# Drains of the matmul banks ahead of weight splits, and the attention bursts of the odd layer three eighths later in their unit

## The chip, the cores and the metric

The kernel runs on one core of one Trainium2 chip. The metric is the time of one execution in microseconds on the device; the kernel before has a median of 748.38 us of three runs (748.29 to 749.49). TensorE is called PE in the rows below, VectorE DVE, ScalarE ACT, GpSimd POOL and SyncE SP.

## The reference

Two layers over 256 tokens of 1024 features, in fp32, each an attention and a squared-ReLU MLP, with RMS norms and residual adds. The even layer joins neighbourhood attention (8 heads) and latent attention (8 heads), the odd layer mixes three dilated windows for 16 heads:

```python
for layer in range(DEPTH):                       # DEPTH = 2
    xn = rms_norm(x, norm_mix[layer])
    if layer % 2 == 0:
        x = x + even_mixer(xn, ev_w_in[e], ev_rpb[e], ev_q_norm[e], ev_w_uq[e],
                           ev_kv_norm[e], ev_w_ukv[e], ev_w_o[e], cos_r, sin_r)
    else:
        x = x + odd_mixer(xn, od_w_in[o], od_w_o[o], cos_f, sin_f)
    x = x + sq_relu_mlp(rms_norm(x, norm_mlp[layer]), mlp_w1[layer], mlp_w2[layer])
return rms_norm(x, norm_final)

def odd_mixer(xn, w_in, w_o, cos_f, sin_f):
    hcat = (xn @ w_in).reshape(b, s, DIL_GROUPS, 3, DIL_HEADS, HEAD_DIM)
    q = apply_rope(hcat[:, :, :, 0], cos_f, sin_f)
    k = apply_rope(hcat[:, :, :, 1], cos_f, sin_f)
    v = hcat[:, :, :, 2]
    return dilated_attention(q, k, v) @ w_o      # masked softmax per window, mixed by denominators
```

## The kernel before

The four stages follow one another: the even attention layer (about 0 to 110 us), its MLP (to 300), the odd attention layer (to 565) and the last MLP.

Each product of two fp32 matrices is done as three or two matmuls of halves: every operand is split into a rounded part and the rest. The weights come from HBM by SyncE's DMAs into four buffers `raw`. A weight is then split in four pieces: ScalarE casts (`whi`, line 176), VectorE subtracts (`wlo`, line 177), into three buffers. `weight()` loads four weights ahead and splits two ahead. The function `split` does the same two steps for activations, and so lines 176 and 177 also stand for the results of attention: `oa` and `ob` are the two halves of what a mix leaves in a bank.

TensorE's results lie in eight PSUM banks, four of tag "acc" and four of tag "w". A matmul into a new bank waits until the last result in that bank has been emptied. What empties banks (the *drains*) runs on ScalarE and VectorE as well, behind and between the weight pieces: `joined` (lines 193 and 194) copies and adds the two halves of a projection, line 932 copies turned probabilities (`pts`), lines 848, 851 and 852 scale the values (`v`), line 666 copies the latent layer's values (`vml`), line 722 or 736 copies turned probabilities of the even layer.

A scheduler puts the instructions of each engine in order. Each has a priority that falls with its place in the code; `tc.high_priority(n)` raises what stands under it by n places. TensorE's order follows the written code for the most part.

The odd layer has eight units. A unit is 12 *half steps* (`qk_steps`: two batches of rows by three blocks f by two halves of the depth, a new weight at half steps 0, 4 and 8) and four *value steps* (two weights). Beside the matmuls of unit u stands one *burst*, that of unit u - 1: `mix` of unit u - 3 (lines 942 and 947), `turn` of unit u - 2's first probabilities (12 transpositions, line 929, into two banks), `scores` of unit u - 1 (lines 201 and 907) and between its two kinds the other `turn`. A burst so opens five "acc" banks one after the other, and the half steps open one each two. The softmax of these scores (lines 913 to 917) follows on VectorE and ScalarE.

Of the kernel before, what the change touches and what calls it, by code (L numbers as in the profile page):

```python
# [38 lines left out]
SPLIT_AHEAD = 2  # L39
WPARTS = 4  # L40
NORM_PRIO = 300


@with_exitstack
def trunk(ctx, tc, a, out):
# [27 lines left out]
    def halves(z):  # L73

        return (z[:, 0, :], z[:, 1, :]) if len(z.shape) == 3 else (z[:, :, 0, :], z[:, :, 1, :])
# [99 lines left out]
    def split(hi, lo, src, eng=None):  # L175
        a = nc.scalar.copy(hi, src).ins  # L176
        return a, (eng or nc.vector).tensor_tensor(lo, src, hi.bitcast(F32), op=ALU.subtract).ins  # L177
# [25 lines left out]
    def weave(main, side, lead=0):  # L203

        done = 0
        for i, step in enumerate(main):
            step()
            while done < len(side) and done * (len(main) - lead) < (i + 1 - lead) * len(side):
                side[done]()
                done += 1  # L210

    def tok(t):
        return slice(t * P, (t + 1) * P)
# [258 lines left out]
    def even(ep):  # L472
# [124 lines left out]
        def qk_steps(c):  # L597
            hold = {}

            def step(f, half):  # L600
                if not hold:
                    hold["w"], hold["p"] = weight(), bank("acc" if c else "w")
                (wh, wl), pq = hold["w"], two(hold["p"])
                for k in range(4 * half, 4 * half + 4):
                    ws = slice(k * 256 + f * P, k * 256 + f * P + P)
                    mm3(pq[:, f], wh[:, ws], wl[:, ws], *halves(xT[:, k]), k == 0, k == KT - 1)
                if f == 1 and half == 1:
                    qk[c] = pair_tile(ep, 2, "qk", 2, "qk")
                    q32 = scratch([2, T], "q32")
                    nc.vector.tensor_tensor(q32, pq, both, op=ALU.mult)  # L610
                    split(*halves(qk[c]), q32)

            return [lambda f=f, h=h: step(f, h) for f in range(2) for h in range(2)]
# [13 lines left out]
        def query_steps():  # L627
            hold = {}

            def step(m):  # L630
                if not hold:
                    hold["w"] = latent_weight("q", "mq")
                wh, wl = hold["w"]
                pq = two(bank("acc"))
                for j in range(2):
                    for k in range(2):
                        c = slice(k * D + (2 * m + j) * P, k * D + (2 * m + j + 1) * P)
                        mm3(pq[:, j], wh[:, c], wl[:, c], cT_h[:, k], cT_l[:, k], k == 0, k == 1)
                q32 = scratch([2, T], "qm")
                nc.vector.tensor_tensor(q32, pq, turns, op=ALU.mult)  # L640
                split(*halves(mT["q"][:, 2 * m:2 * m + 2]), q32)

            return [lambda m=m: step(m) for m in range(4)]

        def key_value_steps():
            hold = {}

            def keys(b):
                if not hold:
                    hold["w"] = latent_weight("k", "mk")  # L650
                    for j, rows in enumerate((slice(64, P), slice(0, 64))):
                        nc.sync.dma_start(by_parity(mT["k"])[rows, j].bitcast(F32), cT[rows, 3].bitcast(F32).unsqueeze(1).broadcast_to([64, 4, 2, T]))
                wh, wl = hold["w"]
                pk = two(bank("acc"))
                for m in range(2):
                    c = slice((2 * b + m) * P, (2 * b + m + 1) * P)
                    mm3(pk[:, m], wh[:, c], wl[:, c], cT_h[:, 2], cT_l[:, 2], True, True)
                for j, rows in enumerate((slice(0, 64), slice(64, P))):
                    o = by_parity(mT["k"])[rows, j, 2 * b:2 * b + 2]
                    split(o[:, :, 0], o[:, :, 1], pk[rows])  # L660

            def values(t):
                wh, wl = hold["w"]
                pv = bank("acc")
                mm3(pv, cT_h[:, 2, tok(t)], cT_l[:, 2, tok(t)], wh[:, 512:D], wl[:, 512:D], True, True)
                nc.any.tensor_copy(out=vml[:, t], in_=pv)

            return [lambda b=b: keys(b) for b in range(2)] + [lambda t=t: values(t) for t in range(NT)]

# [55 lines left out]
        def turn_pair(hp):  # L725

            pt, pts = [bank("w") for _ in range(2)], [scratch([8, 64], "pts") for _ in range(2)]
            for t in range(NT):
                pp = probs.pop(2 * hp + t)
                for b in range(4):  # L730
                    for r in range(2):
                        rows, at = slice(64 * r, 64 * r + 64), slice((4 * t + b) * 64, (4 * t + b) * 64 + 64)
                        nc.tensor.transpose(pt[r][:, at], pp[rows, b // 2, (b % 2) * P:(b % 2 + 1) * P], ident[rows, rows])
                turned[2 * hp + t] = [(slice(64 * r, 64 * r + 64), lambda b, t=t, r=r: pts[r][:, 4 * t + b, :]) for r in range(2)]
            for r in range(2):
                nc.any.tensor_copy(out=pts[r], in_=pt[r].rearrange("p (b n) -> p b n", b=8))

        def mix(*pairs):
            kind, _, hp = items[2 * pairs[0]]
            if mixed[kind] is None:  # L740
                mixed[kind] = quarter_pair("ob")
            v = (vna, vml)[kind]
            pvo = bank("acc" if pairs[0] < 2 else "w")
            for i, m in enumerate(pairs):
                for t in range(NT):
                    pts, o = turned.pop(2 * m + t), i * T + t * P
                    for own, block in pts:
                        for kk in range(NT):
                            for j in range(2):
                                h = 2 * (hp + i) + j  # L750
                                nc.tensor.matmul(pvo[64 * j:64 * j + 64, o + own.start:o + own.stop], v[:, kk, h * 64:(h + 1) * 64],  # L751
                                                 block(2 * j + kk), start=kk == 0, stop=kk == NT - 1)
            n = len(pairs)
            split(*halves(mixed[kind][:, hp:hp + n]), pvo[:, 0:n * T].rearrange("p (i n) -> p i n", i=n))

        def attention():

# [57 lines left out]
    def odd(op, xT, s):  # L815
# [15 lines left out]
        def value_steps(d):  # L831

            wt, acc = [], {}

            def gemm(i, half):
                if len(wt) <= half:
                    wt.append(weight())
                if half == 0:
                    acc[i] = bank("acc")
                pq = acc[i]  # L840
                wh, wl = wt[half]
                for k in range(4):
                    ws = slice(k * 384, k * 384 + 384)
                    kk = 4 * half + k
                    mm3(pq[:, 0:384], xh[:, kk, tok(i)], xl[:, kk, tok(i)], wh[:, ws], wl[:, ws], kk == 0, kk == KT - 1)
            def out(i):
                pq, ri = acc[i], column(r[0], i)
                nc.vector.tensor_scalar(d["v0"][:, i, :], pq[:, 0:P], ri, None, ALU.mult)
                for c in range(2):
                    rows = slice(64 * c, 64 * c + 64)  # L850
                    nc.scalar.activation(d["v12"][0:64, 2 * i + c, :], pq[rows, P:2 * P], AF.Copy, scale=ri[rows])  # L851
                    nc.scalar.activation(d["v12"][64:P, 2 * i + c, :], pq[rows, 2 * P:3 * P], AF.Copy, scale=ri[rows])  # L852

            return [lambda i=i, h=h: gemm(i, h) for i in range(NT) for h in range(2)], [lambda i=i: out(i) for i in range(NT)]

        def qk_steps(d):
# [4 lines left out]
            def gemm(b, f, half):  # L861
# [6 lines left out]
                    ws = slice((f * KT + k) * P, (f * KT + k + 1) * P)  # L868
                    mm2(pq, wh[:, ws], wl[:, ws], xT[:, k], k == 0, k == KT - 1)
                if half == 1:  # L870
                    joined(s[:, f], pq)
                if f == 1 and half == 1:
                    rope(b, s)

# [45 lines left out]
        def turn(u, i, tag):  # L920
# [7 lines left out]
                        rows = slice(64 * r, 64 * r + 64)  # L928
                        nc.tensor.transpose(pt[r][:, at], pp[rows, b * P:(b + 1) * P], ident[rows, rows])
            pts = turned[u, i] = op.tile([P, 6, P], F32, tag="pts", name="pts", bufs=2)  # L930
            for r in range(2):
                nc.any.tensor_copy(out=pts[:, :, 64 * r:64 * r + 64], in_=pt[r][:, 0:384].rearrange("p (b n) -> p b n", b=6))

        def mix(u, d, out_tag):
            pvo = bank(out_tag)
            for i in range(NT):
# [6 lines left out]
                for c in range(2):  # L943
                    qs = slice(64 * c, 64 * c + 64)
                    for j in range(2):
                        cs = slice(64 * j, 64 * j + 64)
                        nc.tensor.matmul(pvo[cs, at + 64 * c:at + 64 * c + 64], d["v12"][:, 2 * i + c, cs], pts[:, 3 * j + 2, qs],
                                         start=False, stop=c == 1)
            split(*halves(mixed[u // 4][:, u % 4]), pvo[:, 0:T])

        units = [unit_tiles(0)]
        d = units[0]
# [27 lines left out]

        for u in range(1, 8):
            units.append(unit_tiles(u))
            placed = {3 if u == 1 else 1: burst(u - 1)}
            if u == 7:
                placed[13] = burst(7)
            beside(qk_steps(units[u]) + all_values(units[u]), placed)
# [119 lines left out]
```

## Time and profile before

| what | value |
|---|---|
| median of three runs | 748.38 us |
| the profiled execution | 749.12 us, its span 747.3 us |
| PE busy | 731.1 us, 98% |
| DVE busy | 537.2 us, 72% |
| ACT busy | 464.2 us, 62% |
| DMA | mean 183 GB/s |

Times in the rows are microseconds from the span's start. A timeline row gives start, duration, engine, source line, operation, what it writes and reads, the count, and in brackets the idle time ahead of it with what ended it. Neighbours of one kind are merged in one row.

### The profile page before, as it was taken

To read this page: it belongs to the slowest core of one execution; us is meant where nothing else is said; L and a number is where in the kernel's file an instruction comes from. 1 tells how busy PE (TensorE), PEld (TensorE's weight loads), DVE (VectorE), ACT (ScalarE), POOL (GpSimd) and SP (SyncE) were. 2 spreads that over 40 slices of the span, in tenths; PEclk is the share of its full clock that TensorE was granted. 3 is DMA by queue.
4 is the path that set the end of the run, shared out by engine and by line. 5 is a ranking of instruction groups with operands and counts; after the bars stand their busy time and mean duration, and the time that the engine had idled before them with its cause. 6 is when DMAs were issued, how large, how long until landed. Compare 5 with 4: busy or idle time off the path is not lost.

```text
span 747.3 us, 12828 instructions
## 1 busy us (share of the span) xinstructions
PE 731.1 (98%) x4932; PEld 641.7 (86%) x4932; DVE 537.2 (72%) x1111; ACT 464.2 (62%) x1043; POOL 6.0 (1%) x16
## 2 busy tenths in 40 slices
PE   8998999999999999999999999999999999999996
PEld 5898998888888888888989889888898888888885
DVE  6698869665665666998777777787669665665664
ACT  7689967544544547766686676866757554554541
POOL 0100000000000000000000000000000000000000
PEclk9999999999999999999999999999999999999998
DMA  8966334555556545675545665456364655455501
GB/s 279 344 209 219 117 123 157 200 195 197 183 184 210 184 142 169 212 247 177 190 167 173 199 210 172 159 189 200 99 242 170 210 184 187 175 202 180 182 33 56
DMA packets 28108, 136.89 MB, mean 183 GB/s; under 512 B 4496, under 2 KB 7056, under 8 KB 14992
## 3 DMA queue, kind: packets, MB, share of 16 engines
q1 hardware_dynamic: 27760, 135.81, 53.5%
q8 instruction: 38, 0.62, 0.3%
q10 hardware_dynamic: 288, 0.28, 0.1%
q14 instruction: 22, 0.18, 0.1%
HBM read 127.68 MB, written 1.05 MB: 172 GB/s over the span
## 4 chain that ended last, share of the span: by engine, by line
PE 85%; ACT 7%; DVE 3%; DMA 2%; issue 1%; SPq 0%; POOLq 0%; POOL 0%; DVEq 0%
PE w L186 16%; PE acc L180 13%; PE acc L181 13%; PE acc L182 13%; PE acc L186 10%; PE w L187 8%; PE acc L187 5%; ACT whi L176 3%; DVE wlo L177 1%; DMA raw<-in_w_v 1%; PE w L751 1%; DMA bias<-in_rpb 1%; ACT v L851 1%; ACT v L852 1%; PE w L907 1%
## 5 line engine op out<-in xcount | busy, mean ns | idle before, releaser
L177 DVE TENSOR_TENSOR wlo<-raw,whi 128x512 fp32r<-128x512 f32 (+3 forms) x488 | 303.5, 664 | 72.1 <-ACT whi L176 70.8
L176 ACT CAST whi<-raw 128x512 fp32r<-128x512 f32 (+3 forms) x488 | 264.5, 602 | 80.7 <-issue 70.3
L186 PE MATMUL w<-xT,whi 128*128 128x512 f32 x512 | 179.4, 394 | 0.0
L186 PE MATMUL acc<-xT,whi 128*128 128x512 f32 x384 | 134.6, 397 | 0.0
L187 PE MATMUL w<-xT,wlo 128*128 128x256 f32 x512 | 132.8, 280 | 0.0
L186 PEld LDWEIGHTS w<-xT,whi 128*128 128x128 f32 x512 | 93.6, 187 | 18.3
L187 PEld LDWEIGHTS w<-xT,wlo 128*128 128x128 f32 x512 | 96.1, 188 | 5.5
L187 PE MATMUL acc<-xT,wlo 128*128 128x256 f32 x384 | 99.9, 280 | 0.0
L180 PE MATMUL acc<-whi,h 128*128 128x512 f32 x250 | 98.4, 393 | 0.0
L181 PE MATMUL acc<-wlo,h 128*128 128x512 f32 x250 | 97.8, 391 | 0.0
L182 PE MATMUL acc<-whi,h 128*128 128x512 f32 x250 | 97.4, 390 | 0.0
L186 PEld LDWEIGHTS acc<-xT,whi 128*128 128x128 f32 x384 | 69.8, 187 | 13.6
L193 ACT COPY up<-w 128x256 f32<-128x256 f32 x64 | 23.9, 373 | 88.4 <-PE w L186 88.4
L187 PEld LDWEIGHTS acc<-xT,wlo 128*128 128x128 f32 x384 | 72.1, 188 | 3.7
L194 DVE TENSOR_TENSOR up<-up,w 128x256 f32<-128x256 f32 x64 | 26.9, 420 | 62.6 <-ACT up L193 61.9
L181 PE MATMUL acc<-wlo,xT 128*128 128x384 f32 (+2 forms) x160 | 56.3, 352 | 0.6 <-DVE wlo L177 0.6
L180 PE MATMUL acc<-whi,xT 128*128 128x384 f32 (+2 forms) x160 | 56.2, 351 | 0.7 <-ACT whi L176 0.5
L182 PEld LDWEIGHTS acc<-whi,h 128*128 128x128 f32 x250 | 47.0, 188 | 10.2
L182 PE MATMUL acc<-whi,xT 128*128 128x384 f32 (+2 forms) x160 | 55.5, 347 | 0.0
L181 PEld LDWEIGHTS acc<-wlo,h 128*128 128x128 f32 x250 | 47.0, 188 | 9.8
L180 PEld LDWEIGHTS acc<-whi,h 128*128 128x128 f32 x250 | 46.9, 188 | 9.1
L193 ACT COPY qk<-acc 128x256 f32<-128x256 f32 x48 | 17.6, 367 | 31.8 <-PE acc L186 31.6
(202 smaller groups left out, 1021.6 us busy)
## 6 DMA issues: line engine op xcount, KB each, us to landing
raw<-in_w SPq DMA_DIRECT2D x64, 1024.0 KB, 4.8
raw<-in_w_oqk SPq DMA_DIRECT2D x24, 1024.0 KB, 5.0
raw<-in_w_ov SPq DMA_DIRECT2D x16, 768.0 KB, 4.8
sw<-qk SPq DMA_DIRECT2D x96, 64.0 KB, 3.1
raw<-in_w_qk SPq DMA_DIRECT2D x4, 1024.0 KB, 11.4
raw<-in_w_oe SPq DMA_DIRECT2D x4, 1024.0 KB, 7.6
raw<-in_w_oo SPq DMA_DIRECT2D x4, 1024.0 KB, 5.1
bias<-in_rpb SPq DMA_DIRECT2D x8, 256.0 KB, 5.5
```

The source lines that it names most:

```text
L176: a = nc.scalar.copy(hi, src).ins
L177: return a, (eng or nc.vector).tensor_tensor(lo, src, hi.bitcast(F32), op=ALU.subtract).ins
L180: nc.tensor.matmul(o, sh, mh, start=first, stop=False)
L181: nc.tensor.matmul(o, sh, ml, start=False, stop=False)
L182: nc.tensor.matmul(o, sl, mh, start=False, stop=last)
L186: both = lambda: nc.tensor.matmul(o, sh, m.rearrange("p v n -> p (v n)"), start=first, stop=last)
L187: low = lambda: nc.tensor.matmul(o[:, 0:T], sl, m[:, 0, :], start=False, stop=False)
L193: nc.scalar.copy(dst, o[:, T:2 * T])
L194: nc.vector.tensor_tensor(dst, dst, o[:, 0:T], op=ALU.add)
L751: nc.tensor.matmul(pvo[64 * j:64 * j + 64, o + own.start:o + own.stop], v[:, kk, h * 64:(h + 1) * 64], block(2 * j + kk), start=kk == 0, s ...
L851: nc.scalar.activation(d["v12"][0:64, 2 * i + c, :], pq[rows, P:2 * P], AF.Copy, scale=ri[rows])
L852: nc.scalar.activation(d["v12"][64:P, 2 * i + c, :], pq[rows, 2 * P:3 * P], AF.Copy, scale=ri[rows])
```

## The change

The change adds a priority of 80 places (`DRAIN_PRIO`, as `soon()`) to the operations that empty banks in both attention layers. It also moves the bursts of the odd layer: that beside unit u stood behind half step 1 (3 for u = 1) and stands behind half step 5 for all.

```diff
+DRAIN_PRIO = 80
+    def soon():
+        return tc.high_priority(DRAIN_PRIO)
 # even layer: scaled query products q32 and qm, key splits, the value copy
+                    with soon():
+                        nc.vector.tensor_tensor(q32, pq, both, op=ALU.mult)
+                with soon():
+                    nc.vector.tensor_tensor(q32, pq, turns, op=ALU.mult)
+                    with soon():
+                        split(o[:, :, 0], o[:, :, 1], pk[rows])
+                with soon():
+                    nc.any.tensor_copy(out=vml[:, t], in_=pv)
 # turned probabilities and mixes, in both layers (the even one shown)
+            with soon():
+                for r in range(2):
+                    nc.any.tensor_copy(out=pts[r], in_=pt[r].rearrange("p (b n) -> p b n", b=8))
+            with soon():
+                split(*halves(mixed[kind][:, hp:hp + n]), pvo[:, 0:n * T].rearrange("p (i n) -> p i n", i=n))
 # odd layer: values, projections, bursts
+                with soon():
                     nc.vector.tensor_scalar(d["v0"][:, i, :], pq[:, 0:P], ri, None, ALU.mult)
...
                 if half == 1:
-                    joined(s[:, f], pq)
+                    with soon():
+                        joined(s[:, f], pq)
...
-            placed = {3 if u == 1 else 1: burst(u - 1)}
+            placed = {5: burst(u - 1)}
             if u == 7:
                 placed[13] = burst(7)
```

What this does to the order, at three places. The new kernel's line numbers are larger by 1 (lines 176 to 194), 9 or 10 (even layer) and 12 to 14 (odd layer). First ScalarE in a unit of the odd layer, before the change: `whi_4412` is the weight of the unit's half steps 8 to 11, `qk` a projection's copy, `oa` the mix, `pts` the turned probabilities, line 915 the softmax.

```order
318 L852 ACTIVATE v12_3853<-acc_4192,rstd_3302 64x128
319 L176 CAST whi_4412<-raw_4163 128x512
320 L193 COPY qk_4239<-acc_4240 128x256
321 L176 CAST whi_4412<-raw_4163 128x512
322 L176 CAST oa_3221<-acc_4259 128x256
323 L932 COPY pts_4292<-acc_4278 128x6x64
324 L932 COPY pts_4292<-acc_4279 128x6x64
325 L932 COPY pts_4325<-acc_4311 128x6x64
326 L915 ACTIVATE pp_4345,dz_4347<-sn_4344,dmn_4346 128x384
```

And the same place after it, where `whi_4472` is the unit's first value weight:

```order
325 L177 CAST whi_4291<-raw_4163 128x512 x2
326 L194 COPY qk_4239<-acc_4240 128x256
327 L194 COPY qk_4239<-acc_4259 128x256
328 L177 CAST whi_4472<-raw_4227 128x384 x4
329 L194 COPY qk_4301<-acc_4302 128x256
330 L177 CAST oa_3221<-acc_4321 128x256
331 L946 COPY pts_4354<-acc_4340 128x6x64
332 L946 COPY pts_4387<-acc_4373 128x6x64
333 L928 ACTIVATE pp_4407,dz_4409<-sn_4406,dmn_4408 128x384
```

Two projections and a whole value weight now come ahead of the mix, and of the turned probabilities two copies of four are ScalarE's instead of three.

Second, VectorE at the same place, before:

```order
432 L177 TENSOR_TENSOR wlo_4230<-raw_4138,whi_4229 128x512 x2
433 L177 TENSOR_TENSOR wlo_4413<-raw_4163,whi_4412 128x512
434 L194 TENSOR_TENSOR qk_4239<-qk_4239,acc_4240 128x256
435 L177 TENSOR_TENSOR wlo_4413<-raw_4163,whi_4412 128x512 x2
436 L177 TENSOR_TENSOR oa_3221<-acc_4259,oa_3221 128x256
437 L177 TENSOR_TENSOR wlo_4413<-raw_4163,whi_4412 128x512
438 L932 COPY pts_4325<-acc_4312 128x6x64
439 L913 ISA sn_4344,dmn_4346<-w_4295,mask_3217 128x384
```

and after:

```order
438 L195 TENSOR_TENSOR qk_4239<-qk_4239,acc_4259 128x256
439 L178 TENSOR_TENSOR wlo_4473<-raw_4227,whi_4472 128x384 x4
440 L893 TENSOR_TENSOR r1_4279<-qk_4239,cosT_3215 128x512
441 L195 TENSOR_TENSOR qk_4301<-qk_4301,acc_4302 128x256
442 L178 TENSOR_TENSOR oa_3221<-acc_4321,oa_3221 128x256
443 L946 COPY pts_4354<-acc_4341 128x6x64
444 L946 COPY pts_4387<-acc_4374 128x6x64
445 L926 ISA sn_4406,dmn_4408<-w_4357,mask_3217 128x384
446 L926 ISA dmn_4408 128x1
447 L894 TENSOR_TENSOR sw_4278<-sw_4278,sinT_3216 128x512
448 L926 ISA sn_4415,dmn_4417<-w_4358,mask_3217 128x384
```

No weight stands between the projection's sum and the mix's low half any more, and a product of the rope with the exchanged halves (`sw`, brought by a DMA) stands between the first two masks of the softmax.

Third, ScalarE in the even layer, where the keys (`mk`) of the latent heads are split, before:

```order
65 L176 CAST qk_868<-q32_869 128x2x256
66 L176 CAST mk_873<-acc_888 64x2x256
67 L176 CAST whi_902<-raw_724 128x512 x2
68 L176 CAST mk_873<-acc_888 64x2x256
69 L176 CAST whi_902<-raw_724 128x512 x2
70 L176 CAST mq_899<-qm_925 128x2x256
71 L176 CAST mk_873<-acc_929 64x2x256
72 L176 CAST oa_393<-acc_940 128x256
73 L736 COPY pts_961<-w_959 128x512
74 L736 COPY pts_962<-w_960 128x512
75 L666 COPY vml_392<-acc_1036 128x512
76 L176 CAST mk_873<-acc_929 64x2x256
```

and after:

```order
66 L177 CAST mk_873<-acc_888 64x2x256
67 L177 CAST mk_873<-acc_929 64x2x256
68 L722 ACTIVATE pp_842<-pp_842,rz_846 128x256
69 L177 CAST qk_868<-q32_869 128x2x256
70 L177 CAST oa_393<-acc_940 128x256
71 L177 CAST mk_873<-acc_929 64x2x256
72 L177 CAST whi_902<-raw_724 128x512 x4
73 L177 CAST mq_899<-qm_925 128x2x256
74 L746 COPY pts_961<-w_959 128x512
75 L746 COPY pts_962<-w_960 128x512
76 L675 COPY vml_392<-acc_1036 128x512
```

The four key casts stand ahead of the weight's four pieces, the query's split behind three of them, and `vml` behind the same two copies as before. SyncE's and GpSimd's orders are the same in both kernels.

More of the change, by code (lines that the diff above doesn't have):

```diff
@@ L609, in step @@
                     q32 = scratch([2, T], "q32")
-                    nc.vector.tensor_tensor(q32, pq, both, op=ALU.mult)
+                    with soon():
+                        nc.vector.tensor_tensor(q32, pq, both, op=ALU.mult)
                     split(*halves(qk[c]), q32)
@@ L639, in step @@
                 q32 = scratch([2, T], "qm")
-                nc.vector.tensor_tensor(q32, pq, turns, op=ALU.mult)
+                with soon():
+                    nc.vector.tensor_tensor(q32, pq, turns, op=ALU.mult)
                 split(*halves(mT["q"][:, 2 * m:2 * m + 2]), q32)
@@ L659, in keys @@
                     o = by_parity(mT["k"])[rows, j, 2 * b:2 * b + 2]
-                    split(o[:, :, 0], o[:, :, 1], pk[rows])
+                    with soon():
+                        split(o[:, :, 0], o[:, :, 1], pk[rows])
             def values(t):
@@ L665, in values @@
                 mm3(pv, cT_h[:, 2, tok(t)], cT_l[:, 2, tok(t)], wh[:, 512:D], wl[:, 512:D], True, True)
-                nc.any.tensor_copy(out=vml[:, t], in_=pv)
+                with soon():
+                    nc.any.tensor_copy(out=vml[:, t], in_=pv)
             return [lambda b=b: keys(b) for b in range(2)] + [lambda t=t: values(t) for t in range(NT)]
@@ L734, in turn_pair @@
                 turned[2 * hp + t] = [(slice(64 * r, 64 * r + 64), lambda b, t=t, r=r: pts[r][:, 4 * t + b, :]) for r in range(2)]
-            for r in range(2):
-                nc.any.tensor_copy(out=pts[r], in_=pt[r].rearrange("p (b n) -> p b n", b=8))
+            with soon():
+                for r in range(2):
+                    nc.any.tensor_copy(out=pts[r], in_=pt[r].rearrange("p (b n) -> p b n", b=8))
         def mix(*pairs):
@@ L753, in mix @@
             n = len(pairs)
-            split(*halves(mixed[kind][:, hp:hp + n]), pvo[:, 0:n * T].rearrange("p (i n) -> p i n", i=n))
+            with soon():
+                split(*halves(mixed[kind][:, hp:hp + n]), pvo[:, 0:n * T].rearrange("p (i n) -> p i n", i=n))
         def attention():
@@ L847, in out @@
                 pq, ri = acc[i], column(r[0], i)
[L848 to L852, printed above, removed]
+                with soon():
+                    nc.vector.tensor_scalar(d["v0"][:, i, :], pq[:, 0:P], ri, None, ALU.mult)
+                    for c in range(2):
+                        rows = slice(64 * c, 64 * c + 64)
+                        nc.scalar.activation(d["v12"][0:64, 2 * i + c, :], pq[rows, P:2 * P], AF.Copy, scale=ri[rows])
+                        nc.scalar.activation(d["v12"][64:P, 2 * i + c, :], pq[rows, 2 * P:3 * P], AF.Copy, scale=ri[rows])
             return [lambda i=i, h=h: gemm(i, h) for i in range(NT) for h in range(2)], [lambda i=i: out(i) for i in range(NT)]
@@ L930, in turn @@
             pts = turned[u, i] = op.tile([P, 6, P], F32, tag="pts", name="pts", bufs=2)
-            for r in range(2):
-                nc.any.tensor_copy(out=pts[:, :, 64 * r:64 * r + 64], in_=pt[r][:, 0:384].rearrange("p (b n) -> p b n", b=6))
+            with soon():
+                for r in range(2):
+                    nc.any.tensor_copy(out=pts[:, :, 64 * r:64 * r + 64], in_=pt[r][:, 0:384].rearrange("p (b n) -> p b n", b=6))
         def mix(u, d, out_tag):
@@ L948, in mix @@
                                          start=False, stop=c == 1)
-            split(*halves(mixed[u // 4][:, u % 4]), pvo[:, 0:T])
+            with soon():
+                split(*halves(mixed[u // 4][:, u % 4]), pvo[:, 0:T])
         units = [unit_tiles(0)]
```

## The prediction

> **What bounds the kernel now.** I read the page first, then the list of what TensorE waits for, then its busy time stretch by stretch, and last the timeline of one period on three engines.
>
> ```profile
> PE 731.1 (98%) x4932; PEld 641.7 (86%) x4932; DVE 537.2 (72%) x1111; ACT 464.2 (62%) x1043; POOL 6.0 (1%) x16
> ```
>
> TensorE (PE) is busy 98% of the span, so time can only come out of its gaps or its matmuls, and the change touches no matmul. The list of its waits says who ends the gaps (columns: total us, times, longest):
>
> ```profile
> PE acc L929 <- DVE oa L177: 3.0, 4, 0.7
> PE acc L180 <- ACT vml L666: 1.9, 1, 1.9
> ...
> PE acc L929 <- ACT pts L932: 1.1, 1, 1.1
> PE acc L929 <- DVE ob L177: 0.7, 1, 0.7
> ...
> PE acc L180 <- ACT v L852: 0.5, 1, 0.5
> ...
> PE w L907 <- DVE k L886: 0.2, 1, 0.2
> ```
>
> All are in the two attention layers, and nearly all name an operation that empties a bank. In the table by stretches (each engine's busy us, with its instruction count, then clock and DMA):
>
> ```profile
> 60.00:80.00 20.00, 18.06 (x207) 16.40 (x207) 18.14 (x45) 19.60 (x48) 0.00 (x0) 1.00 0.46 167
> ...
> 344.00:354.00 10.00, 8.86 (x104) 7.95 (x103) 7.98 (x16) 8.88 (x20) 0.00 (x0) 1.00 0.68 255
> 354.00:505.60 151.60, 147.92 (x1221) 134.07 (x1221) 117.30 (x261) 106.64 (x255) 0.00 (x0) 1.00 0.56 183
> ```
>
> The even layer lacks 1.94 us in one place; the first burst with transpositions 1.14; the five units after it 3.68 together. The clock is 1.00 throughout. One steady period on TensorE:
>
> ```profile
> 406.66 0.40 PE L186 MATMUL acc<-xT,whi 128*128 128x512 f32 x1
> ...
> 409.60 0.66 PE L942 MATMUL acc<-pts,v 128*64 128x128 f32 x8
> ...
> 411.09 0.58 PE L929 MATMUL acc<-ident,pp 64*128 64x64 f32 x12
> 411.49 0.96 PE L201 MATMUL w<-q 64*128 64x256 f32 x12
> 412.29 0.21 PE L929 MATMUL acc<-ident,pp 64*128 64x64 f32 x1
> 413.24 0.58 PE L929 MATMUL acc<-ident,pp 64*128 64x64 f32 x11 [0.74 <-DVE oa L177]
> 413.75 0.69 PE L907 MATMUL w<-k,q 64*64 64x64 f32 x32
> ```
>
> The burst starts with the mix at 409.60. Its first block of 12 transpositions (411.09) takes 0.40 from start to start; the second, begun at 412.29, takes until 413.75, that is 1.46. So a burst loses 1.46 - 0.40 = 1.06 us, more than the 0.74 printed as idle, since tails of matmuls count as busy. The second bank of this block is the fifth "acc" bank in a row (mix result, two, two) and there are four, so it needs the mix's own bank back. That bank is emptied by oa, on ScalarE (high part) and VectorE (rest):
>
> ```profile
> 411.09 0.62 ACT L176 CAST whi<-raw 128x512 fp32r<-128x512 f32 x1
> 411.62 0.37 ACT L176 CAST oa<-acc 128x256 fp32r<-128x256 f32 x1
> ```
>
> ```profile
> 411.23 0.42 DVE L194 TENSOR_TENSOR qk<-qk,acc 128x256 f32<-128x256 f32 x1 [0.58 <-ACT qk L193]
> 411.56 1.29 DVE L177 TENSOR_TENSOR wlo<-raw,whi 128x512 fp32r<-128x512 f32 x2
> 412.77 0.42 DVE L177 TENSOR_TENSOR oa<-acc,oa 128x256 fp32r<-128x256 f32 x1
> ```
>
> The mix is through at about 411.1. One cast of a weight stands before oa's high part, two subtractions of a weight (1.29 us) before its low part; the bank is free at 413.19. Without them it would be 411.1 + 0.37 + 0.42 = 411.9, ahead of 412.3. The engines are not full (72% and 62%): the order in their queues is at fault.
>
> **The change, part by part.** It adds and removes no instruction, and the queues of SyncE and GpSimd keep their order. What moves:
>
> *Odd bursts after half step 5 instead of 1, with drains preferred.* In a unit's time (0 at its first half step; a half step is (409.60 - 406.66)/2 = 1.47 us, an upper value, as this holds a switch of work): the weights still split at the burst before (the unit's third block) now have four half steps to finish. In their place come the four pieces of the first value weight, whose buffer is free after half step 3, at 5.9, and half step 3's own copy goes first. Four such casts take 1.75 us on ScalarE (timeline), and a subtraction on VectorE has a mean of 553 ns (the groups by line and shape, of the odd layer):
>
> ```profile
> 423.37 1.75 ACT L176 CAST whi<-raw 128x384 fp32r<-128x384 f32 x4
> ```
>
> ```profile
> L177 DVE TENSOR_TENSOR wlo<-raw,whi 128x384 fp32r<-128x384 f32 x56 | 29.7, 553 | 0.0
> ```
>
> ScalarE: copy to 6.3, casts to about 8.0, then half step 5's copy 8.8 to 9.2, then it is free. VectorE: four subtractions at about 0.5 apart, done at 8.8, the rope product after them (0.6) at 9.4, half step 5's sum at 9.8. The mix runs from 8.8 to 10.3; oa's high part then is done at 10.7, its low part at 11.2. The second block's second bank is wanted at 8.8 + (412.29 - 409.60) = 11.5. So there is 0.3 us to spare, and the stall goes whole: 5 bursts by 1.06 = 5.3 us. Both ends: 0, were the split still in front (the row of 1.29 us), and 5.3.
>
> What is late next: the second value weight. Its pieces stand behind the softmax now. These rows show the softmax's last step, the second value step's start, and the price of an exchange of halves (KB each, us to landing):
>
> ```profile
> 419.53 0.61 ACT L917 ACTIVATE pp<-pp,drz 128x384 f32<-128x384 f32 x1
> ```
>
> ```profile
> 430.63 0.34 PE L180 MATMUL acc<-whi,xT 128*128 128x384 f32 x1
> ```
>
> ```profile
> sw<-qk SPq DMA_DIRECT2D x96, 64.0 KB, 3.1
> ```
>
> The softmax ends 420.1 - 409.6 = 10.5 us after a burst's start, 9.4 without the stall, so at 18.2; the casts follow to 20.0, the first piece is whole by 19.5. The second value step wants it at 430.63 - 406.66 - 1.06 = 22.9. Some 3 us are spare, so I cost it at nothing; if the cover is gone, each us of lateness costs one in each of seven units. On VectorE the product with the exchanged halves now stands inside the softmax: the exchange starts after half step 3's sum (6.7), its four parts are issued within some 2 us, an estimate, and the last lands at about 11.6; VectorE gets to it behind the first mask at about 13. That costs nothing either, with 1.4 us spare. The loads ahead of it in SyncE's queue wait for buffers that come free by then.
>
> *The first burst with transpositions* stalls on a copy of a turned block instead:
>
> ```profile
> 351.23 0.21 PE L929 MATMUL acc<-ident,pp 64*128 64x64 f32 x1
> 352.58 0.58 PE L929 MATMUL acc<-ident,pp 64*128 64x64 f32 x11 [1.14 <-ACT pts L932]
> ```
>
> From 351.23 to 352.58 it is 1.35 where the steady burst has 0.95 (412.29 to 413.24), so it loses 1.06 + 0.40 = 1.46. There is no mix here, so the bank wanted there is that of half step 5, emptied at 9.4 to 9.8 against a need at about 9.7: nearly all is won, 1.46. In the very first burst the wait of 0.2 for k goes, as it lies two half steps later.
>
> *The tail of the odd layer.*
>
> ```profile
> 526.77 0.59 PE L929 MATMUL acc<-ident,pp 64*128 64x64 f32 x12
> 527.54 0.44 PE L180 MATMUL acc<-whi,xT 128*128 128x384 f32 x1 [0.19 <-ACT pts L932]
> ```
>
> ```profile
> 535.67 0.28 PE L181 MATMUL acc<-oa,whi 128*128 128x256 f32 x1
> 535.79 0.28 PE L182 MATMUL acc<-oa,wlo 128*128 128x256 f32 x1
> 536.53 0.39 PE L180 MATMUL acc<-oa,whi 128*128 128x256 f32 x1 [0.46 <-ACT v L852]
> ```
>
> The second gap is 0.74 - 0.12 = 0.62 (neighbours here start 0.12 apart); the value evictions that end it lie among the softmax's steps and go ahead of them now. The first is a mix drain behind four evictions, which themselves now count as drains, so I leave a stall of about its size there. The tail gives 0.9 at most, 0 at least; I take 0.8.
>
> *The even layer.* Its one gap:
>
> ```profile
> 66.11 0.39 PE L181 MATMUL acc<-wlo,c 128*128 128x512 f32 x1
> 66.34 0.39 PE L182 MATMUL acc<-whi,c 128*128 128x512 f32 x1
> 68.66 0.39 PE L180 MATMUL acc<-c,whi 128*128 128x256 f32 x1 [1.94 <-ACT vml L666]
> ...
> 70.89 0.28 PE L180 MATMUL acc<-c,whi 128*128 128x256 f32 x1
> ```
>
> ```profile
> 62.85 1.14 ACT L176 CAST whi<-raw 128x512 fp32r<-128x512 f32 x2
> ...
> 68.01 0.60 ACT L666 COPY vml<-acc 128x512 f32<-128x512 f32 x1
> ```
>
> From 66.34 the next would start at 66.57 (0.23 after it, as it started 0.23 after its own neighbour), so 2.09 us are lost. In the new order the key copies pass the casts, but the four casts still stand ahead of vml, and ScalarE is busy 19.60 of 20 us here, so this copy hardly comes sooner. TensorE instead gets other matmuls to run meanwhile. Against that the last pair of scores now waits about 0.9 for its query split, which stands behind the key copies. Walking through the new order with these durations, the third query block starts at about 69.4 where it was 70.9: 1.5. The ends are -1 (only the loss) and 2.09; I take 1.5, nearer to the gap's own rows.
>
> **Sum:** 5.3 + 1.5 + 0.2 + 0.8 + 1.5 = 9.3 us. The profiled execution took 749.12 us with a span of 747.3; that gives 739.8. The median of the runs is 748.38, 0.74 lower, which gives 739.1. I forecast 739.3.
>
> **The rivals.**
>
> *Half the stalls stay.* The slack of 0.3 us per burst is smaller than one subtraction (553 ns) or the copy ahead of it. If the value weight's load or buffer comes one piece later, oa's low part waits by 0.3 to 0.6 us, and the burst keeps about half its loss: 5 by 0.5 less, the even layer at 0: 9.3 - 2.5 - 1.5 = 5.3, so about 743. For it speaks that four subtractions now stand right ahead of the drains on VectorE, against it that their buffer is free three us before the mix begins.
>
> *The bank shortage stays.* Five banks from four are wanted in a row, and that does not change; the gap may move to another bank of the burst and keep its size. Then only the even layer and the tail are won or nothing: 746 to 748.4, no measurable change. Against it: the bank is held up to 413.19 of which 1.29 us is a weight's subtraction, so it is the time the bank is held and not the number that makes the gap. The Trainium skill, "Perfetto Trace Analysis", section "Optimization Strategy", says that the same gap repeating on the engine that should be saturated can mean that there isn't enough PSUM for the next tile. By that rule alone the change, which adds no bank, would bring nothing; the rows agree that a bank is what is waited for, and disagree that a fifth one is needed.
>
> *Slower: the second value weight comes late.* If the exchange lands late, everything behind its product on VectorE stands: masks, reciprocals, and through them ScalarE's softmax and the second value weight. From 1.4 us of lateness on the softmax slips, from 4.4 on TensorE waits at the second value step. To end above 748.38 + 1.5 it must wait (9.3 + 1.5)/7 = 1.5 us in each unit, so the exchange must be late by 5.9. With waits of 2 us: 739.3 + 14 = 753. For it speaks that nothing but the value steps covers this weight any more; against it the landing in 3.1 us.
>
> **How the numbers follow.** Forecast 0.62; half the stalls 0.2; shortage stays 0.1; slower 0.08. What a measurement of this kernel can tell from no change is about 0.2%, 1.5 us. Faster: forecast, half, and a part of the third, 0.84; same 0.08; slower 0.08. The range: at the low end every term at its upper value (5.3, 1.5, 0.2, 0.9 and 2.1 is 10.0) and 0.8 more for waits that the idle column hides: 748.38 - 10.8 = 737.6, at the high end beyond the half case, 745.2.
>
> **What would show it.** In the profile after, the list of TensorE's waits has no line of L942 (the transpositions' new number) waiting for oa, and units of 29.3 instead of 30.33 us; in 344 to 506 TensorE lacks under 1 us where it lacked 4.8. A line of transpositions waiting for oa at 0.2 to 0.6 means the second case; waiting for other drains at 0.7, the third; a line of value matmuls (L181) waiting for whi or wlo, the fourth. The even layer's 60 to 80 shows 0.4 to 0.6 us idle if its term holds. I would be wrong above all if a stall that the trace now hides behind the old gaps comes out once they are gone.

## The result and the profile after

The changed kernel has a median of 740.85 us over five runs, against 748.29 us for five runs of the kernel before: a ratio of 0.9903 (95% interval 0.9887 to 0.9919). A second comparison, with runs of both kernels side by side, gave 741.11 against 750.30 us, 0.9875 (0.9857 to 0.9893). The two profiled spans are 747.3 and 739.0 us, 8.3 apart. (A burst moves by four of a unit's sixteen steps; the title's three eighths are the place where it now stands.)

The whole list of what TensorE waits for after the change (total us, times, longest):

```profile
PE acc L91 <- DVE warm L85: 1.2, 1, 1.2
PE acc L181 <- ACT whi L177: 0.9, 1, 0.9
PE w L729 <- ACT pp L722: 0.4, 1, 0.4
PE acc L182 <- DVE wlo L178: 0.4, 2, 0.2
PE acc L181 <- ACT v L864: 0.3, 1, 0.3
PE w L942 <- DVE ob L178: 0.2, 1, 0.2
PE w L202 <- ACT qk L177: 0.2, 1, 0.2
PE acc L942 <- DVE ob L178: 0.2, 1, 0.2
```

The waits for oa, vml and the turned probabilities are gone. The waits for whi and wlo all end before 17.3 us of the span, ahead of everything that the change moves; they are not the late value weight of the prediction's slower case. The busy time by stretches says the same (columns as before):

```profile
60.00:80.00 20.00, 19.40 (x216) 17.41 (x215) 17.70 (x43) 19.66 (x48) 0.00 (x0) 1.00 0.41 151
...
344.00:354.00 10.00, 10.00 (x58) 8.70 (x56) 7.87 (x16) 8.42 (x19) 0.00 (x0) 1.00 0.68 233
354.00:500.00 146.00, 146.00 (x1207) 133.10 (x1208) 119.78 (x267) 105.84 (x250) 0.00 (x0) 1.00 0.58 191
```

From 344 to 500 us TensorE has no gap. One steady burst after the change, on TensorE and VectorE:

```profile
411.19 0.66 PE L956 MATMUL acc<-pts,v 128*64 128x128 f32 x8
...
412.69 0.58 PE L942 MATMUL acc<-ident,pp 64*128 64x64 f32 x12
413.08 0.96 PE L202 MATMUL w<-q 64*128 64x256 f32 x12
413.88 0.53 PE L942 MATMUL acc<-ident,pp 64*128 64x64 f32 x12
414.35 0.69 PE L920 MATMUL w<-k,q 64*64 64x64 f32 x32
```

```profile
411.89 0.41 DVE L195 TENSOR_TENSOR qk<-qk,acc 128x256 f32<-128x256 f32 x1
413.20 0.42 DVE L178 TENSOR_TENSOR oa<-acc,oa 128x256 fp32r<-128x256 f32 x1 [0.90 <-ACT oa L177]
```

oa's low part ends at 413.62, and VectorE even stood idle for 0.90 us ahead of it. The second transpositions start at 413.88 and take 0.47 to the next kind of matmul, where they took 1.46.

The same landmarks of TensorE's timeline, read in both profiles, show where the 8.3 us lie. Up to the key's transposition TensorE's instructions stand in the same order in both kernels; units are counted from their first half step.

| stretch | before, us | after, us | difference |
|---|---|---|---|
| start to the key's transposition | 42.75 | 42.22 | -0.53 |
| from there to the first MLP | 70.60 | 69.98 | -0.62 |
| first MLP to the odd layer's first half step | 188.84 | 188.83 | -0.01 |
| odd, first stretch and unit 1 | 44.90 | 44.43 | -0.47 |
| unit 2 | 29.25 | 27.85 | -1.40 |
| units 3 to 7, up to the last value steps | 143.16 | 138.19 | -4.97 |
| from there to the last MLP | 41.79 | 41.49 | -0.30 |
| last MLP | 179.79 | 179.80 | +0.01 |

A unit repeats every 29.33 us where it took 30.33.

### The profile page after: what moved, and what is told of

It is laid out like the page before. It is cut to its first block, busy times and chain, and to the rows that moved or that the text cites. A ratio compares the mean times of both kernels' runs of the same rounds, so it can differ in the third digit from the quotient of the medians.

```text
span 739.0 us, 12836 instructions
## 1 busy us (share of the span) xinstructions
PE 729.3 (99%) x4932; PEld 641.4 (87%) x4932; DVE 538.2 (73%) x1116; ACT 463.5 (63%) x1038; POOL 6.0 (1%) x16
## 4 chain that ended last, share of the span: by engine, by line
PE 89%; ACT 4%; DMA 3%; DVE 2%; issue 1%; SPq 1%; POOLq 0%; POOL 0%; ACTq 0%; DVEq 0%
PE w L187 16%; PE acc L181 13%; PE acc L182 13%; PE acc L183 13%; PE acc L187 11%; PE w L188 8%; PE acc L188 6%; PE w L761 1%; DMA raw<-in_w_v 1%; PE w L202 1%; DMA bias<-in_rpb 1%; DVE wlo L178 1%; PE acc L942 1%; PE w L729 1%; PE w L181 1%
## 5 line engine op out<-in xcount | busy, mean ns | idle before, releaser
L182 PEld LDWEIGHTS acc<-wlo,xT 128*128 128x128 f32 x160 | 30.1, 188 | 3.1 <-DVE wlo L178 2.1
```

Source lines behind the costliest of these rows:

```text
L182: nc.tensor.matmul(o, sh, ml, start=False, stop=False)
```

## The experiments

**The two halves of the change.** First the priority alone:

```diff
-            placed = {5: burst(u - 1)}
+            placed = {3 if u == 1 else 1: burst(u - 1)}
```

> The priority for drains alone; the bursts stay behind half step 1 (3 for the first). If the place of the burst carries the gain in the odd layer: units of 30.33 us as before, the transpositions still wait 0.7 us for oa four times, and only the even layer (0.6 us) and the tail (0.3 us) are won: about 747.4 us. If the priority carries it: units of about 29.3 us, 741 to 742 us.

743.99 us, ratio 0.9924 (0.9894 to 0.9954). Then the place alone, in the kernel before:

```diff
-            placed = {3 if u == 1 else 1: burst(u - 1)}
+            placed = {5: burst(u - 1)}
```

> The bursts behind half step 5 for every unit, no priority for drains. If the place carries the gain in the odd layer: units of 29.33 us and no wait for oa, the even layer as before with its wait of 1.9 us for vml, about 741.8 us. If the priority is needed there: units of 30 us or more, 746 us or more.

744.68 us, ratio 0.9934 (0.9911 to 0.9957). Each was expected to fail where the other carries the gain, and neither did. From unit 3 on, the priority alone gives units of 29.33 us (first one 29.34), and so does the place alone (but for the third unit, 29.99). The 5 us of the steady units are won by either, once. Unit 2 separates them: 29.26 us with the priority alone, 27.85 with the place alone. The place alone also has the 44.42 us of the stretch up to unit 2, where the priority alone has 44.88. So 1.4 + 0.5 us are the place's own. With the place alone the drain is early, as in the changed kernel: oa ends 2.44 us after its burst's start.

Why the priority helps at the old place is seen in its burst. TensorE, VectorE and ScalarE, priority alone:

```profile
411.67 0.54 PE L942 MATMUL acc<-ident,pp 64*128 64x64 f32 x12
412.14 0.69 PE L920 MATMUL w<-k,q 64*64 64x64 f32 x32
```

```profile
410.90 1.29 DVE L178 TENSOR_TENSOR wlo<-raw,whi 128x512 fp32r<-128x512 f32 x2
412.11 0.42 DVE L178 TENSOR_TENSOR oa<-acc,oa 128x256 fp32r<-128x256 f32 x1
```

```profile
411.09 0.86 ACT L946 COPY pts<-acc 128x384 f32<-128x384 f32 x2
```

oa is not a bit sooner: two weight subtractions still stand ahead of it, and it ends at 412.53, 3.54 us after the burst's start (408.99), before the change 3.59. Yet the transpositions at 411.67 do not wait. In the compiled program their second bank is no longer the mix's but that of the first transpositions, whose first copy on ScalarE, begun at 411.09, is through by then. The priority changed which bank was handed out, and left this drain where it was.

**Which bank, without any priority.** Two edits of the kernel before tell the bank from the queue. One lets the burst open with the first transpositions:

```diff
-                if u > 1:
-                    mix(u - 2, units[u - 2], "acc")
                 if u > 0:
                     turn(u - 1, 0, "acc")
+                if u > 1:
+                    mix(u - 2, units[u - 2], "acc")
```

> The kernel before, in which a burst opens with the first transpositions and the mix follows; no priority, same place. The second transpositions' second bank is then that of the first transpositions, emptied by a copy on ScalarE, and oa's low part stays behind three weight subtractions on VectorE. If it is the bank that counts: the stall goes with oa as late as before, units of 29.3 to 29.5 us, about 743 us. If any drain is late because weight splits stand ahead: a wait of 0.5 us or more for the copy, units of 29.8 us or more.

745.30 us, ratio 0.9942 (0.9925 to 0.996); steady units of 29.56 us. TensorE and VectorE in it:

```profile
411.51 0.54 PE L929 MATMUL acc<-ident,pp 64*128 64x64 f32 x12
411.98 0.69 PE L907 MATMUL w<-k,q 64*64 64x64 f32 x32
```

```profile
410.57 1.89 DVE L177 TENSOR_TENSOR wlo<-raw,whi 128x512 fp32r<-128x512 f32 x3
412.38 0.42 DVE L177 TENSOR_TENSOR oa<-acc,oa 128x256 fp32r<-128x256 f32 x1
```

Three subtractions stand ahead of oa, it ends at 412.80, 1.3 us after the transpositions began, and nobody waits for it. The stall goes though the drain is later (4.20 us after the burst's start at 408.60). What is left, 0.23 us a unit, is nearly all between the first transpositions and the mix (408.60 to 409.21, 0.61 from start to start, where the first transpositions take 0.39 after the change); why is not shown.

The other edit puts the mix into the other tag:

```diff
-                    mix(u - 2, units[u - 2], "acc")
+                    mix(u - 2, units[u - 2], "w")
```

> The kernel before, with the mix of a burst in a bank of the other tag (w) instead of acc. The burst then wants four acc banks and five w banks in a row. If a burst is held up by whichever matmul gets the mix's bank next: the wait for oa moves from the second transpositions to the fourth scores (line 201), which are wanted at about 412.1 in the period shown where oa ends at 413.2: a wait of 0.8 to 1.1 us in each of five units, units of 30.2 to 30.4 us, no gain. If the fifth acc bank is what costs: units of 29.3 us, 743 us.

752.07 us in one run; steady units of 30.73 us, 0.4 more than in the kernel before and above the range that was expected. Its list of waits:

```profile
PE w L201 <- DVE oa L177: 4.1, 4, 1.0
PE w L201 <- DVE ob L177: 2.1, 2, 1.0
```

The wait moved to the fourth scores, which need the fifth bank of that tag, and grew from 0.74 to 1.0 us. So the stall follows the mix's bank, whoever gets it. And five banks from four are no harm by themselves, as the run with the transpositions first shows; harm comes when the bank handed out is the one whose drain stands behind a weight.

**How far behind the half steps.** The changed kernel with the burst behind half step 3, and behind 7:

```diff
-            placed = {5: burst(u - 1)}
+            placed = {3: burst(u - 1)}
```

> The changed kernel with the bursts behind half step 3 instead of 5. If what matters is how long a weight's buffer has been free when the burst comes: the first value weight's buffer comes free just at the burst, its four casts (1.75 us) and four subtractions (about 2.0 us, behind a half step's sum) run during the mix, oa is through some 3.3 us behind the burst's start where it is wanted at 2.7: a wait of 0.5 to 0.6 us for oa in each unit, units of about 29.9 us, 744 us. If it is enough that the weight of half steps 8 to 11 is split by then: units of 29.3 us, 741 us.

743.46 us, ratio 0.9921 (0.9893 to 0.9949); units of 29.52 us.

```diff
-            placed = {5: burst(u - 1)}
+            placed = {7: burst(u - 1)}
```

> The changed kernel with the bursts behind half step 7. If what matters is how long a weight's buffer has been free: the second value weight's buffer comes free just at the burst, and as behind half step 3 the transpositions wait 0.4 to 0.8 us for oa: units of 29.8 to 30.1 us, 744 to 746 us. If only the distance from the unit's start matters: units of 29.3 us, 741 us.

744.07 us, ratio 0.9937 (0.9912 to 0.9962); units of 29.52 to 29.60. Both cost 0.2 us a unit, not 0.5. TensorE and ScalarE with the burst behind half step 3:

```profile
412.40 0.73 PE L942 MATMUL acc<-ident,pp 64*128 64x64 f32 x12
413.06 0.69 PE L920 MATMUL w<-k,q 64*64 64x64 f32 x32
```

```profile
410.09 1.75 ACT L177 CAST whi<-raw 128x384 fp32r<-128x384 f32 x4
411.75 0.37 ACT L177 CAST oa<-acc 128x256 fp32r<-128x256 f32 x1
412.01 0.86 ACT L946 COPY pts<-acc 128x384 f32<-128x384 f32 x2
```

The four casts of the weight whose buffer has just come free stand ahead of the drains, as expected. But here too the program gave the second transpositions the bank of the first, so they wait only for the first copy, begun at 412.01, and for some 0.2 us: the block takes 0.66 where it takes 0.47 after the change. So the phase of the weight buffers counts, and the bank decides how much. The medians lie further above the changed kernel's than five times 0.2 us, and part of that lies in the tail: in these profiles TensorE waits there 1.2 us for k (line 920) with the burst behind half step 3, and 0.6 us for ob with it behind 7.

One steady burst of each kernel, side by side. The bank is that of the compiled program. The end of oa is counted from the burst's start; the second bank is wanted about 2.7 us after it (2.9 with the transpositions first).

| kernel | second transpositions get | oa ends, us | their block takes, us |
|---|---|---|---|
| before | the mix's bank | 3.59 | 1.46 |
| changed | the mix's bank | 2.43 | 0.47 |
| place alone | the mix's bank | 2.44 | 0.46 |
| priority alone | the first transpositions' bank | 3.54 | 0.47 |
| transpositions first | the first transpositions' bank | 4.20 | 0.47 |
| behind half step 3 | the first transpositions' bank | 3.22 | 0.66 |
| behind half step 7 | the first transpositions' bank | 3.65 | 0.73 |

Of these only the kernel before has both, the mix's bank and a drain later than the need, and only it has the long stall.

**The even layer.** The priority there alone, in the kernel before (the line is one of six so kept, the four places of the odd layer lose theirs):

```diff
+                with soon():
+                    nc.any.tensor_copy(out=vml[:, t], in_=pv)
```

> The kernel before with the priority for drains in the even layer alone. Units of 30.3 us and the waits for oa stay. If the even layer's part of the priority is worth what its profile shows: the 1.9 us wait for vml goes, waits of 0.4 to 1.3 us for the softmax come, the even layer is shorter by 0.3 to 1.5 us (by up to 2.5 where the clock falls after the long wait before): 746 to 748 us against the kernel before. If it is worth nothing: the same time.

749.24 against 749.98 us, ratio 0.9994 (0.9982 to 1.0005): no difference that can be told from none. The units of 30.33 us and the waits for oa stay, the wait for vml goes. The opposite, the changed kernel with the priority in the odd layer alone, ran beside the changed kernel once more:

```diff
-                with soon():
+                with tc.high_priority(0):
                     nc.any.tensor_copy(out=vml[:, t], in_=pv)
```

> The changed kernel with the priority in the odd layer alone; the even layer has the order of the kernel before, with its wait of 1.9 us for vml. If the even layer's part brings what the forecast had for it (1.5 us): 1.5 us slower than the changed kernel on the same chip. If it only trades this wait for waits on the softmax behind a late bias DMA: the same as the changed kernel within 0.8 us; and the clock may fall behind the 1.9 us wait in some executions (1.4 us more).

743.32 us, ratio 0.9901 (0.9881 to 0.9922); units of 29.33 us, and the wait of 1.9 us for vml is there.

> The changed kernel once more, beside the run above. Units of 29.33 us; if the 8.3 us between the two profiles is what the change brings: a ratio of 0.989 to 0.990 to the kernel before; if 0.5 us of it is how the start of the profiled executions fell: 0.990 to 0.991. The even layer from the key's transposition to the MLP takes 70 us where the bias lands in time, up to 71.8 where it is late by 1.5 us.

741.11 us, 0.9875 (0.9857 to 0.9893), units of 29.33 us. Here the even layer's priority is worth 2.2 us (743.32 - 741.11), there 0.7 (749.98 - 749.24), and the intervals of the ratios reach 0.9 to 1.6 us either way. The profiles show that this part differs from execution to execution. With the priority in the even layer, TensorE waited longest for the softmax (1.3 us) in the two executions in which VectorE waited longest for a bias DMA (1.9 and 2.1 us in total); in the execution with the priority alone (first row VectorE's list, second TensorE's):

```profile
DVE sn L714 <- DMA bias<-in_rpb: 1.9, 2, 1.0
```

```profile
PE w L742 <- ACT pp L722: 1.3, 1, 1.3
```

From the key's transposition to the first MLP, six executions with this order took 69.98, 71.53, 70.51, 69.99, 71.77 and 70.54 us; five with the order of before took 70.60, 72.70, 70.78, 71.22 and 73.18. The means are 70.7 and 71.7, but the two groups overlap, so 1.0 us is no firm number.

**More of the same.** A priority of 300 instead of 80 in the changed kernel:

```diff
-DRAIN_PRIO = 80
+DRAIN_PRIO = 300
```

> The changed kernel with a priority of 300 places instead of 80. In the even layer the copies of turned probabilities pass the four casts of the output weight, and vml is copied sooner. If drains are still late there: the even layer is 0.4 to 1 us shorter, 740 us. If the rest of the even layer hangs on the softmax and its bias DMA: the same time as the changed kernel, 740.9 us.

742.65 us, ratio 0.9909 (0.9894 to 0.9924), no faster than the changed kernel. TensorE's wait of 0.4 us for the softmax at line 729 is not in its list any more; one of 0.4 at line 742 is, and the even layer takes 70.1 us (42.84 to 112.91). From unit 7 to the last MLP it takes 63.4 us where the changed kernel takes 62.4, with a wait of 0.6 us for ob there. No version ran faster than the changed kernel.

## Why the prediction was right, and where it was not

*The forecast* was 739.3 us, the measured median is 740.85; the sum was 9.3 us, the profiles are 8.3 apart, of which 0.5 fell before the change acts. This start is not the change's: over the executions the key's transposition came between 41.5 and 42.8 us, with either order behind it. So the change accounts for 7.8 us of the 8.3, and the half us that brings the profiles nearer to the sum is luck. The signs named for the forecast came: no wait of line 942 for oa, units of 29.33 us, no gap from 344 to 500 us.

*Five steady bursts, 5.3 us:* 4.97. The mechanism as told holds in the changed kernel: its second bank is still the mix's, oa ends 2.43 us after the burst's start (2.4 forecast), the bank is wanted at 2.7, and the 0.3 us to spare are there. The missing 0.3 us are 0.07 in each burst: the second block takes 0.47 us, and the sum had 0.40. That half the stalls stay did not happen, nor did the second value weight come late.

*The reading of the cause was too narrow.* "It needs the mix's own bank back" and "the order in their queues is at fault" were taken as one fact. The runs showed two conditions that have to meet: the bank handed to the second transpositions is the mix's, and oa stands behind a weight. With the transpositions first, the second is fulfilled more than before and there is no stall; after the change the first is fulfilled and there is none. Against the rival of the bank shortage the prediction set the time that the bank is held, and in the changed kernel that is what was mended; that another choice among the same four banks would do as well, it did not see. The rule of the Trainium skill ("Perfetto Trace Analysis", section "Optimization Strategy"), that a repeating gap can mean too little PSUM, is half borne out by these runs: a bank is what was waited for, but no fifth one was needed, since another choice among the four was enough.

*Priority and place* were costed together. They are substitutes in the steady units, so the sum came out, but it does not say what either edit brings alone.

*Unit 2, 1.46 us:* 1.40, the place's alone. *The first burst, 0.2:* 0.47 up to unit 2; part of it was in no row of waits.

*The tail, 0.8 us:* 0.30. The wait of the first output block for the value evictions fell from 0.46 only to 0.3 us, and a wait of the last turned block for ob came in place of that for the copy. I had let the evictions pass the softmax; on ScalarE three of its four exponentials still stand ahead of them (522.28 to 525.62).

*The even layer, 1.5 us:* 0.62 between these two profiles, 1.0 between the means over executions, and 0.7 and 2.2 in the two timed comparisons. Up to where the walk through the new order ended it was nearly right: the third query block starts 26.88 us after the key's transposition (69.10 - 42.22), before the change 28.14 (70.89 - 42.75), which is 1.26 us won. The step that failed is that the walk stopped there and costed nothing behind it. TensorE's next turned probabilities wait for the softmax, and start 0.70 us after their neighbour where neighbours start 0.12 apart: 0.58 us lost.

```profile
72.34 0.44 PE L729 MATMUL w<-ident,pp 128*128 128x128 f32 x2 [0.42 <-ACT pp L722]
```

What the softmax's last step (line 722) stood behind are drains that the change prefers. On VectorE the two query products now go ahead of its reciprocals, on ScalarE the second copy of the values ahead of the step itself:

```profile
69.72 1.28 DVE L647 TENSOR_TENSOR qm<-acc,turns 128x512 f32<-128x512 f32 x2
70.92 0.21 DVE L720 RECIPROCAL rz<-z 128x2 f32<-128x2 f32 x2
```

```profile
71.31 0.58 ACT L675 COPY vml<-acc 128x512 f32<-128x512 f32 x1
71.78 1.71 ACT L722 ACTIVATE pp<-pp,rz 128x256 f32<-128x256 f32 x4
```

Before the change the first reciprocal stood ahead of the products (70.47 and 70.88), and the value copy was VectorE's. The wait of 0.42 to 0.43 us at line 729 is in all six executions with this order and in none with the order of before, so it is not chance; which of the two passings costs how much, no run tells. That the even layer shows 0.60 us idle in 60 to 80 us, as the prediction named for its sign, could not tell a gain of 1.5 from one of 0.6. The prediction also took the bias's landing of one execution as given and left out the clock (below), by which single executions differ. That this part could lose was within its ends, and was not seen.

## What to carry to other kernels

When a matmul waits for a bank, ask two things of the profile: what stands ahead of the drain in its queue, and why this bank and not one that was empty sooner. Either can be mended alone: an early drain won 1.00 us a unit here, and another order of opening the same banks, behind a drain as late as ever, 0.77. A priority is paid for by what it passes, so look for who waits for the work that it passes. A gap that hangs on a DMA's landing should be costed from several executions, not from one.

## What the runs showed that was not expected

Behind a wait of 1.9 us TensorE's granted clock fell in some executions. The kernel with the place alone has the same 1.9 us wait for vml in the even layer as the kernel before. Its busy time in three stretches, the clock in the third column from the right:

```profile
67.20:69.10 1.90, 0.01 (x1) 0.00 (x0) 1.87 (x5) 1.90 (x5) 0.00 (x0) 0.95 0.42 112
69.10:72.50 3.40, 3.35 (x14) 3.26 (x15) 3.28 (x13) 3.09 (x10) 0.00 (x0) 0.52 0.64 258
72.50:76.00 3.50, 3.50 (x30) 3.41 (x30) 3.31 (x9) 3.50 (x9) 0.00 (x0) 1.00 0.00 0
```

For about 3.4 us the clock was 0.52, and the matmuls came 0.21 us apart:

```profile
69.53 0.41 PE L181 MATMUL acc<-c,whi 128*128 128x256 f32 x1
69.74 0.41 PE L182 MATMUL acc<-c,wlo 128*128 128x256 f32 x1
```

In the profile of the kernel before the same matmuls came 0.12 apart (68.88 and 69.00) and the clock stayed at 1.00 behind the same wait. From the end of the wait to the third query block it took 3.64 us here (69.15 to 72.79) and 2.23 there (68.66 to 70.89), 1.4 us more. It happened in two of five executions that had this wait (the other is the priority in the odd layer alone), and in none of the six, with the priority of 80 there, in which the even layer's longest wait was at most 1.3 us. But the length of the wait alone does not decide. In the profile with the priority of 300 the clock was 0.51 from 8.0 to 11.5 us, behind a wait of 1.10 us for whi (up to 7.58); in the changed kernel the same place has a wait of 0.89 us and a clock of 1.00.

The Trainium skill, "TensorE: Matmul & The Clock Gate", section "HAM oscillation — how this bites in real kernels", states as a rule that TensorE should have no idle gaps of more than about 3.4 us. Here the clock fell behind gaps of 1.9 and 1.1 us, in some executions. The 3.4 us at the lower clock agree with the time that the same page of the Trainium skill gives for its return (section "What's actually happening": about 3.4 us of sustained work).

So where the clock falls, the wait for vml costs 1.4 us on top of its 1.9. Two of five executions are too few to say how often that is, and how long a gap must be stays open.
